# Marking two chains as urgent at once: a retention chunk and an attention block

## The chip, the cores and the metric

The kernel runs on one core of a Trainium2 chip. The metric is the time of one execution on the device in microseconds (us); the time of before is the median of three runs. A core has five engines that run side by side, each with its own queue of instructions that it works off in order: TensorE (PE, matmuls and their weight loads, PEld), VectorE (DVE), ScalarE (ACT), GpSimd (POOL) and SyncE (SP, which issues most transfers). An instruction that waits for a semaphore holds up all that is queued behind it on its engine.

## The reference

The kernel computes a decoder of two layers on one sequence of 1024 tokens with 1024 channels, in float32. Each layer has retention heads and differential attention heads side by side:

```python
u = rmsnorm(h, attn_norm[l])
rq, rk, rv, rg, dq, dk, dv = split(u @ w_in[l])
# retention, chunks of 128, 4 heads of 64 (keys) and 128 (values)
s = einsum(q, k) * decay                  # inside a chunk
out = einsum(s, v) + einsum(q * q_decay, state)
state = g_chunk * state + einsum(k * k_decay, v)
# differential attention, 4 heads, blocks of 128 queries, causal, ALiBi
p = softmax(q_j @ k_j.T * scale - slope * dist)      # j = 0, 1
a = p[0] - lam * p[1]
o = a @ v
h = h + concat(retention, attention) @ w_out[l]
h = h + SwiGLU(rmsnorm(h, ffn_norm[l]))
```

with norms of the outputs of both groups, a gate on retention's, and a last rmsnorm behind the second layer.

## The kernel before, in words

One class, `Trunk`, emits the whole program. Activations lie with channels on the partitions. Matmuls that need the accuracy of float32 are done as three products of a high and a low part (the groups L264 to L266, L288 to L290 and L323 to L325 of the profile). The high part is a copy by ACT, the low part a subtraction by DVE, and so nearly each tile that PE reads has first gone through ACT and then through DVE.

The order of the work. PE's queue is written by hand: the kernel runs under `tc.manual_schedule(engines={PE})`, and generators for different parts are woven together (`weave`), so that PE gets matmuls of projections between the matmuls of an attention block or of a retention chunk. In the feed-forward part the other four engines are ordered by hand too. Everywhere else a scheduler orders the instructions of DVE, ACT, POOL and SP when the program is built: of the instructions that could go next it takes them by their place in the program, and one that was emitted under `tc.high_priority()` may go ahead of the others. The order is then fixed; nothing is decided at run time. PSUM banks come from small pools by name (`ps_s`, `ps_t`, `ps_o`, `ps_mm`), and a matmul group waits until the last reader of its bank is done.

An attention block (`att_block`, one head, 128 queries, key range up to `kend` = 128(i+1)) does this, with points between at which other matmuls are woven in:

1. `att_scores` for the second softmax (j = 1): per 512 keys two matmuls (L574, L575) into a bank `ps_s`; L577 on DVE adds the bias and takes the row maximum (it shows as two instructions, the operation and the reading of its accumulator); L580 the maximum of these, L581 on ACT the exponential with the row sum, L582 the reciprocal of the sum.
2. L656 multiplies the reciprocal by minus lambda, L657 on ACT scales the second softmax by it.
3. `att_scores` for the first softmax (j = 0).
4. `att_turn` for the block before: PE transposes its probabilities (L600) into `ps_t`, ACT copies the high part (L605) and DVE subtracts for the low part (L606).
5. L666 on DVE combines the two softmaxes of this block, reading L657's result.

Each second block `att_out` follows, at the next block: L619 and L620 for the high parts and L622 for the low parts (they read L606's tiles), with the output's norm behind it (`att_norm`: L372, L382, L386 to L388 are the steps of its reciprocal root, and L636 applies it). Between the blocks PE works on the projection of the next head, whose results go through `stack` (L522 on ACT, L523 on DVE), or of the values (L546 on ACT, L547 on DVE).

Already urgent before are L605 and L606, L522 and L523, L666, the copies of `split` and `att_out`, and L869 (`add_h`, the residual sum). L577, L580, L581, L582, L656 and L657 are not.

A retention chunk (`retention`, eight chunks of 128) has the scores (`ret_scores`: matmuls into two `ps_s` banks, L793 twice on DVE for the decay, transposes of the keys, L801 on DVE for the keys' decay), the output (L835 and L838 on PE, L840 and L842 on ACT for its square and its copy), the state's increment (L846 on PE, which reads L801's tile) and its update (L853 on DVE, four times). The chunk before is normed meanwhile (`ret_norm`: L372, L382, L386 to L388, then L809, L811 and L817), and PE gets matmuls of the output projection in between, whose sums L869 adds to the residual.

Of the kernel before, what the change touches and what calls it, by code (L numbers as in the profile page):

```python
# [14 lines left out]
AF = mybir.ActivationFunctionType  # L15
ALU = mybir.AluOpType
AX = mybir.AxisListType

P = 128
# [16 lines left out]
NEG = -3.0e38  # L36
# [111 lines left out]
class Trunk:  # L148
# [413 lines left out]
    def att_scores(self, A, i, j, p, z):  # L562
        nc = self.nc
        qs, ks, kb, bias = A["q"][j], A["k"][j], A["kb"][j], A["bias"]
        kend = P * (i + 1)
        nch = (kend + 511) // 512
        mx = self.t("m", 4, [P, 4])
        q = qs[:, P * i:P * i + P]
        for c in range(nch):
            c0 = 512 * c  # L570
            n = min(512, kend - c0)
            nn = max(n, 256)
            ps = self.bank("s")
            nc.tensor.matmul(ps[:, :nn], lhsT=q, rhs=ks[:, c0:c0 + nn], start=True, stop=False)  # L574
            nc.tensor.matmul(ps[:, :nn], lhsT=q, rhs=kb[:, c0:c0 + nn], start=False, stop=True)  # L575
            x0 = c0 - P * i + (T - P)
            nc.vector.tensor_tensor_reduce(  # L577
                out=p[:, c0:c0 + n], in0=ps[:, :n], in1=bias[:, x0:x0 + n], scale=1.0, scalar=NEG,
                op0=ALU.add, op1=ALU.max, accum_out=mx[:, c:c + 1])
        nc.vector.tensor_reduce(out=mx[:, 2:3], in_=mx[:, 0:nch], op=ALU.max, axis=AX.X, negate=True)  # L580
        nc.scalar.activation(p[:, :kend], p[:, :kend], AF.Exp, bias=mx[:, 2:3], accum_out=z[:, j:j + 1])  # L581
        nc.vector.reciprocal(z[:, 2 + j:3 + j], z[:, j:j + 1])  # L582

    def att_turn(self, A, i, p):
        nc = self.nc
# [53 lines left out]
    def att_block(self, l, A, i, prev):  # L639

        nc = self.nc
        kend = P * (i + 1)
        if i < 4:
            pp = self.big("sp")
            p = [pp[:, 0:512], pp[:, 512:1024]]
        else:
            p = [self.big("sp") for _ in range(2)]
        z = self.t("z", 4, [P, 4])
        self.att_scores(A, i, 1, p[1], z)
        yield LAG[0]  # L650
        if self.outs:
            self.att_out(l, *self.outs.pop())
        elif self.norms:
            self.att_norm(l)
        yield i + LAG[1]
        nc.vector.tensor_tensor(out=z[:, 3:4], in0=z[:, 3:4], in1=self.nlam[:, l:l + 1], op=ALU.mult)  # L656
        nc.scalar.mul(p[1][:, :kend], p[1][:, :kend], z[:, 3:4])  # L657
        self.att_scores(A, i, 0, p[0], z)
        yield i + LAG[2]
        if prev:  # L660
            B, k, q = prev
            self.att_turn(B, k, q)
            if k % 2:
                self.outs.append((B, k // 2))
        with self.tc.high_priority():
            nc.vector.scalar_tensor_tensor(out=p[0][:, :kend], in0=p[0][:, :kend], scalar=z[:, 2:3],  # L666
                                           in1=p[1][:, :kend], op0=ALU.mult, op1=ALU.add)
        yield LAG[3]
        self.prev = (A, i, p)
# [108 lines left out]
    def ret_scores(self, x, n):  # L778
        nc = self.nc
        rq, rk = x[0], x[1]  # L780
        cs = slice(P * n, P * n + P)
        buf = self.big("mx")
        sps = [self.bank("s") for _ in range(2)]
        for h in range(4):
            r = slice(64 * (h % 2), 64 * (h % 2) + 64)
            c0 = P * (h // 2)
            nc.tensor.matmul(sps[h % 2][:, c0:c0 + P], lhsT=rk[h // 2][r, cs], rhs=rq[h // 2][r, cs],
                             start=True, stop=True)
        sd = buf[:, 0:512]
        sdv = sd.rearrange("p (a b c) -> p a b c", a=2, b=2)  # L790
        dec = self.tabs[:, 0:512].rearrange("p (a b c) -> p a b c", a=2, b=2)
        for j in range(2):
            nc.vector.tensor_tensor(out=sdv[:, :, j], in0=sps[j][:, 0:256].rearrange("p (a c) -> p a c", a=2),  # L793
                                    in1=dec[:, :, j], op=ALU.mult)
        kd = buf[:, 512:768]
        if n < 7:
            tps = self.bank("t")
            for p in range(2):
                nc.tensor.transpose(out=tps[:, P * p:P * p + P], in_=rk[p][:, cs], identity=self.ident)
            heads = lambda t: t.rearrange("p (h c) -> p h c", h=4)  # L800
            nc.vector.tensor_tensor(out=heads(kd), in0=heads(tps[:, 0:256]),  # L801
                                    in1=heads(self.tabs[:, 768:772]).broadcast_to([P, 4, 64]), op=ALU.mult)
        return sd, kd

    def ret_norm(self, l, x, mix, n, oc, parts):
# [13 lines left out]
    def retention(self, l, x, mix):  # L819
        nc = self.nc  # L820
        rq, rk, rqd, rv, rg = x
        mm = nc.tensor.matmul
        st = self.t("acc", 2, [P, 512])
        nc.gpsimd.memset(st, 0.0)
        state = [st[:, 0:256], st[:, 256:512]]
        sd, kd = self.ret_scores(x, 0)
        yield 2
        late = None
        for n in range(8):
            cs = slice(P * n, P * n + P)  # L830
            rvn = rv[n // 2][:, 512 * (n % 2):512 * (n % 2) + 512]
            ops = self.bank("o")
            for h in range(4):
                o = ops[:, P * h:P * h + P]
                mm(o, lhsT=rvn[:, P * h:P * h + P], rhs=sd[:, P * h:P * h + P], start=True, stop=n == 0)  # L835
                if n:
                    c0 = P * (h % 2)
                    mm(o, lhsT=state[h // 2][:, c0:c0 + P], rhs=rqd[h // 2][:, cs], start=False, stop=True)  # L838
            sq = self.tmp()
            nc.scalar.activation(sq, ops, AF.Square)  # L840
            oc = sd
            nc.scalar.copy(oc, ops)  # L842
            if n < 7:
                kps = self.bank("t")
                for p in range(2):
                    mm(kps[:, 256 * p:256 * p + 256], lhsT=kd[:, P * p:P * p + P], rhs=rvn[:, 256 * p:256 * p + 256],  # L846
                       start=True, stop=True)
                for p in range(2):
                    for j in range(2):
                        r = slice(64 * j, 64 * j + 64)  # L850
                        kv = kps[r, 256 * p + P * j:256 * p + P * j + P]
                        sv = state[p][r, P * j:P * j + P]
                        nc.vector.scalar_tensor_tensor(out=sv, in0=sv, scalar=self.tabs[r, 772 + p:773 + p], in1=kv,  # L853
                                                       op0=ALU.mult, op1=ALU.add)
            yield 3
            if late:
                self.ret_norm(l, x, mix, *late)
            yield 2
            if n < 7:
                sd, kd = self.ret_scores(x, n + 1)  # L860
            late = (n, oc, self.split(sq))
            yield 3
        self.ret_norm(l, x, mix, *late)
        yield 1
# [439 lines left out]
```

## Time and profile before

| | us |
|---|---|
| median of three runs | 2289.64 (2288.03 to 2290.91) |
| the profiled execution, its own time | 2289.0 |
| span in the profile, first to last instruction | 2287.2 |
| PE busy | 2252.3 (98%) |
| DVE busy | 1397.1 (61%) |
| ACT busy | 1009.7 (44%) |
| POOL busy | 732.6 (32%) |

Attention of layer 0 takes about the stretch from 52 to 300 us, retention that from 382 to 451; in layer 1 the same comes some 1126 us later. A row of the view of waits has the engine, the line that waited, what it waited for, the us in total, how often, and the longest. A row of the timeline has start and length in us, the engine, line, operation and tiles, and in brackets the idle time before it with what ended it.

### The profile page before, as it was taken

Reading aid. Unit: us, or ns where it says so; the run is one execution under the profiler, and the core shown is the slowest. Engines: PE = TensorE matmul, PEld = TensorE weight load, DVE = VectorE, ACT = ScalarE, POOL = GpSimd, SP = SyncE. Lnnn points to the kernel's source line nnn. Section 1 sums busy time; section 2 is a strip of 40 time slices with the busy share of each in tenths; the row PEclk is TensorE's granted clock in tenths of the full one; section 3 lists DMA queues with packets and bytes.
Section 4 is the critical chain, followed back from the end, with each engine's and each line's share of the span. In section 5 each row is a group of like instructions: output and inputs, shape, how many; then the busy total and the mean of one; then the engine's idle time right before and its main releaser. Section 6 shows DMA issues by size and latency. Waiting matters only on the chain.

```text
span 2287.2 us, 30638 instructions
## 1 busy us (share of the span) xinstructions
PE 2252.3 (98%) x11328; PEld 1896.9 (83%) x11328; DVE 1397.1 (61%) x2594; ACT 1009.7 (44%) x1906; POOL 732.6 (32%) x592
## 2 busy tenths in 40 slices
PE   8999999999999999999999999999999999999998
PEld 5888898787888888888888888988878888888887
DVE  8777612989534333895567774059884434359855
ACT  5666623445333333543256665234453333344332
POOL 3111212120445455335121112211214555544350
PEclk9999999999999999999999999999999999999999
DMA  4312121112433332653232222112123232346422
GB/s 166 77 47 65 45 94 38 56 56 65 138 104 103 105 107 92 228 180 99 72 101 56 56 65 87 52 38 74 49 95 120 93 115 93 110 148 201 158 65 74
DMA packets 74214, 216.58 MB, mean 95 GB/s; under 512 B 8016, under 2 KB 10064, under 8 KB 74064
## 3 DMA queue, kind: packets, MB, share of 16 engines
q1 hardware_dynamic: 73488, 214.10, 29.0%
q8 instruction: 89, 1.46, 0.3%
q10 hardware_dynamic: 576, 0.52, 0.1%
q14 instruction: 61, 0.50, 0.1%
HBM read 162.16 MB, written 44.04 MB: 90 GB/s over the span
## 4 chain that ended last, share of the span: by engine, by line
PE 81%; DVE 13%; DMA 2%; ACT 2%; issue 2%; POOL 0%; SPq 0%; DVEq 0%; ACTq 0%; POOLq 0%
PE ps_mm L264 7%; PE ps_mm L265 7%; PE ps_mm L266 7%; PE ps_mm L289 7%; PE ps_mm L288 7%; PE ps_mm L290 7%; PE ps_s L265 4%; PE ps_s L264 4%; PE ps_s L266 4%; PE ps_mm L323 3%; PE ps_mm L324 3%; PE ps_mm L325 3%; PE ps_t L265 2%; PE ps_t L264 2%; PE ps_t L266 2%
## 5 line engine op out<-in xcount | busy, mean ns | idle before, releaser
L241 POOL TENSOR_TENSOR w<-wr,w 128x512 fp32r<-128x512 f32 x262 | 366.7, 1413 | 444.6 <-ACT w L240 426.5
L281 POOL TENSOR_TENSOR w<-wr,w 128x512 fp32r<-128x512 f32 x140 | 186.4, 1338 | 576.9 <-ACT w L280 519.7
L288 PE MATMUL ps_mm<-u,w 128*128 128x512 f32 (+1 forms) x735 | 296.1, 403 | 0.0
L289 PE MATMUL ps_mm<-u,w 128*128 128x512 f32 (+1 forms) x735 | 287.2, 391 | 2.3 <-DVE u L450 2.3
L290 PE MATMUL ps_mm<-u,w 128*128 128x512 f32 (+1 forms) x735 | 286.4, 390 | 0.0
L240 ACT CAST w<-wr 128x512 fp32r<-128x512 f32 x312 | 187.5, 619 | 132.9 <-DVE wr L911 72.5
L264 PE MATMUL ps_mm<-u,w 128*128 128x512 f32 x432 | 168.6, 390 | 0.4 <-DVE a L869 0.3
L266 PE MATMUL ps_mm<-u,w 128*128 128x512 f32 x432 | 168.1, 389 | 0.0
L265 PE MATMUL ps_mm<-u,w 128*128 128x512 f32 x432 | 168.1, 389 | 0.0
L290 PEld LDWEIGHTS ps_mm<-u,w 128*128 128x128 f32 x735 | 138.0, 188 | 30.1
L289 PEld LDWEIGHTS ps_mm<-u,w 128*128 128x128 f32 x735 | 138.6, 189 | 25.7 <-DVE u L450 3.0
L288 PEld LDWEIGHTS ps_mm<-u,w 128*128 128x128 f32 x735 | 138.3, 188 | 23.8
L960 ACT COPY t<-ps_mm 128x512 f32<-128x512 f32 x76 | 44.7, 588 | 240.2 <-PE ps_mm L266 240.2
L280 ACT CAST w<-wr 128x512 fp32r<-128x512 f32 x140 | 85.8, 620 | 128.2 <-PE ps_t L289 39.6
L323 PE MATMUL ps_mm<-w,u 128*128 128x256 f32 x448 | 128.7, 287 | 0.0
L325 PE MATMUL ps_mm<-w,u 128*128 128x256 f32 x448 | 127.6, 285 | 0.0
L324 PE MATMUL ps_mm<-w,u 128*128 128x256 f32 x448 | 127.5, 285 | 0.0
L241 POOL TENSOR_TENSOR w<-t,w 128x512 fp32r<-128x512 f32 x48 | 64.7, 1348 | 193.6 <-ACT w L240 193.5
L577 DVE CUSTOM_DVE_ANT_0 sp<-ps_s,wr 128x512 f32<-128x512 f32 (+2 forms) x192 | 102.9, 552 | 32.2 <-PE ps_s L575 31.3
L581 ACT ACTIVATE sp<-sp,m 128x256 f32<-128x256 f32 (+7 forms) x128 | 99.2, 775 | 50.2 <-DVE m L580 49.4
L869 DVE TENSOR_TENSOR a<-a,ps_mm 128x512 f32<-128x512 f32 (+1 forms) x148 | 98.7, 667 | 29.2 <-PE ps_mm L266 16.2
L909 DVE TENSOR_TENSOR t<-wr,wr 128x512 f32<-128x512 f32 x46 | 34.5, 751 | 116.3 <-DMA wr<-wts 115.5
(390 smaller groups left out, 5915.9 us busy)
## 6 DMA issues: line engine op xcount, KB each, us to landing
wr<-wts SPq DMA_DIRECT2D x190, 512.0 KB, 3.7
mx<-s_fast SPq DMA_DIRECT2D x56, 512.0 KB, 5.0
s_fast<-mx SPq DMA_DIRECT2D x48, 512.0 KB, 4.9
kb<-ka SPq DMA_DIRECT2D x64, 128.0 KB, 2.3
s_rest<-mx SPq DMA_DIRECT2D x12, 512.0 KB, 2.9
kb<-wts SPq DMA_DIRECT2D x12, 512.0 KB, 5.5
mx<-s_rest SPq DMA_DIRECT2D x12, 512.0 KB, 3.2
a<-xT SPq DMA_DIRECT2D x16, 256.0 KB, 5.4
```

Source lines behind the costliest of these rows:

```text
L240: nc.scalar.copy(h, src)
L241: (eng or nc.gpsimd).tensor_tensor(out=o, in0=src, in1=h.bitcast(F32), op=ALU.subtract)
L264: mm(ps, lhsT=wh[:, c], rhs=bh, start=first and i == 0, stop=False, skip_group_check=True)
L265: mm(ps, lhsT=wh[:, c], rhs=bl, start=False, stop=False, skip_group_check=True)
L266: mm(ps, lhsT=wl[:, c], rhs=bh, start=False, stop=i == 3, skip_group_check=True)
L281: nc.gpsimd.tensor_tensor(out=o, in0=raw[:, cols], in1=h.bitcast(F32), op=ALU.subtract)
L288: mm(out, lhsT=lh, rhs=rh, start=first, stop=False)
L289: mm(out, lhsT=lh, rhs=rl, start=False, stop=False)
L290: mm(out, lhsT=ll, rhs=rh, start=False, stop=last)
L323: mm(o, lhsT=uh, rhs=wh, start=k == 0, stop=False)
L324: mm(o, lhsT=uh, rhs=wl, start=False, stop=False)
L325: mm(o, lhsT=ul, rhs=wh, start=False, stop=k == KT - 1)
```

## The change

The change wraps the remaining instructions of the two chains in `tc.high_priority()`. In attention these are L577, L580, L581, L582, L656 and L657; in retention L793, L801, L840, L842 and L853. Since L606, L523, L666 and L869 were urgent before, instructions that used to stand behind these now have the same standing, and their place in the program decides. Nothing is added or removed on any engine, and the orders of PE and SP are the same.

```diff
@@ att_scores
-            nc.vector.tensor_tensor_reduce(
-                out=p[:, c0:c0 + n], in0=ps[:, :n], in1=bias[:, x0:x0 + n], scale=1.0, scalar=NEG,
-                op0=ALU.add, op1=ALU.max, accum_out=mx[:, c:c + 1])
-        nc.vector.tensor_reduce(out=mx[:, 2:3], in_=mx[:, 0:nch], op=ALU.max, axis=AX.X, negate=True)
-        nc.scalar.activation(p[:, :kend], p[:, :kend], AF.Exp, bias=mx[:, 2:3], accum_out=z[:, j:j + 1])
-        nc.vector.reciprocal(z[:, 2 + j:3 + j], z[:, j:j + 1])
+            with self.tc.high_priority():
+                nc.vector.tensor_tensor_reduce(
+                    out=p[:, c0:c0 + n], in0=ps[:, :n], in1=bias[:, x0:x0 + n], scale=1.0, scalar=NEG,
+                    op0=ALU.add, op1=ALU.max, accum_out=mx[:, c:c + 1])
+        with self.tc.high_priority():
+            nc.vector.tensor_reduce(out=mx[:, 2:3], in_=mx[:, 0:nch], op=ALU.max, axis=AX.X, negate=True)
+            nc.scalar.activation(p[:, :kend], p[:, :kend], AF.Exp, bias=mx[:, 2:3], accum_out=z[:, j:j + 1])
+            nc.vector.reciprocal(z[:, 2 + j:3 + j], z[:, j:j + 1])
@@ att_block
-        nc.vector.tensor_tensor(out=z[:, 3:4], in0=z[:, 3:4], in1=self.nlam[:, l:l + 1], op=ALU.mult)
-        nc.scalar.mul(p[1][:, :kend], p[1][:, :kend], z[:, 3:4])
+        with self.tc.high_priority():
+            nc.vector.tensor_tensor(out=z[:, 3:4], in0=z[:, 3:4], in1=self.nlam[:, l:l + 1], op=ALU.mult)
+            nc.scalar.mul(p[1][:, :kend], p[1][:, :kend], z[:, 3:4])
@@ ret_scores
-            nc.vector.tensor_tensor(out=sdv[:, :, j], in0=sps[j][:, 0:256].rearrange("p (a c) -> p a c", a=2),
-                                    in1=dec[:, :, j], op=ALU.mult)
+            with self.tc.high_priority():
+                nc.vector.tensor_tensor(out=sdv[:, :, j], in0=sps[j][:, 0:256].rearrange("p (a c) -> p a c", a=2),
+                                        in1=dec[:, :, j], op=ALU.mult)
...
-            nc.vector.tensor_tensor(out=heads(kd), in0=heads(tps[:, 0:256]),
-                                    in1=heads(self.tabs[:, 768:772]).broadcast_to([P, 4, 64]), op=ALU.mult)
+            with self.tc.high_priority():
+                nc.vector.tensor_tensor(out=heads(kd), in0=heads(tps[:, 0:256]),
+                                        in1=heads(self.tabs[:, 768:772]).broadcast_to([P, 4, 64]), op=ALU.mult)
@@ retention
-            nc.scalar.activation(sq, ops, AF.Square)
             oc = sd
-            nc.scalar.copy(oc, ops)
+            with self.tc.high_priority():
+                nc.scalar.activation(sq, ops, AF.Square)
+                nc.scalar.copy(oc, ops)
...
-                        nc.vector.scalar_tensor_tensor(out=sv, in0=sv, scalar=self.tabs[r, 772 + p:773 + p], in1=kv,
-                                                       op0=ALU.mult, op1=ALU.add)
+                        with self.tc.high_priority():
+                            nc.vector.scalar_tensor_tensor(out=sv, in0=sv, scalar=self.tabs[r, 772 + p:773 + p],
+                                                           in1=kv, op0=ALU.mult, op1=ALU.add)
```

The lines of the changed kernel are numbered otherwise: L577 is L578 there, L580 is L582, L582 is L584, L606 is L608, L622 is L624, L636 is L638, L656 is L659, L666 is L669, L793 is L797, L801 is L806, L853 is L860 and L869 is L876. The numbers behind the tiles' names are the program's counts of buffers and banks.

The first place is on DVE at the end of head 0's block 6 in layer 0: `sp_923` and `sp_924` are that block's softmaxes, `sp_1017` that of the block behind it, `a_179_901` and `a_180_902` the low parts of the transposed block before, and `mx_464` the head's output. Before:

```order
L606 TENSOR_TENSOR a_179_901<-ps_t_1000,a_177_899 128x4x128
L606 TENSOR_TENSOR a_180_902<-ps_t_1007,a_178_900 128x2x128
L577 ISA sp_1017,m_1019<-ps_s_1020,wr_467 128x512
L577 ISA m_1019 128x1
L577 ISA sp_1017,m_1019<-ps_s_1024,wr_467 128x512
L577 ISA m_1019 128x1
L523 SCALAR_TENSOR_TENSOR a_105_469<-ps_mm_967,a_105_469 64x512
L582 RECIPROCAL z_925<-z_925 128x1
L580 TENSOR_REDUCE m_1019<-m_1019 128x1
L666 SCALAR_TENSOR_TENSOR sp_923<-sp_923,z_925,sp_924 128x896
```

And in the changed kernel:

```order
L669 SCALAR_TENSOR_TENSOR sp_923<-sp_923,z_925,sp_924 128x896
L578 ISA sp_1017,m_1019<-ps_s_1020,wr_467 128x512
L578 ISA m_1019 128x1
L578 ISA sp_1017,m_1019<-ps_s_1024,wr_467 128x512
L578 ISA m_1019 128x1
L608 TENSOR_TENSOR a_180_902<-ps_t_1007,a_178_900 128x2x128
L582 TENSOR_REDUCE m_1019<-m_1019 128x1
L523 SCALAR_TENSOR_TENSOR a_105_469<-ps_mm_967,a_105_469 64x512
L608 TENSOR_TENSOR a_179_901<-ps_t_1000,a_177_899 128x4x128
```

The combination of the softmaxes has gone from the end to the front, and the first of the two L606 from the front to the end; the instructions up to the last row are the same in both. In head 2's block 6 the same rows change places.

The second place is on DVE at head 1's block 6 in layer 0: `sp_1515` and `sp_1516` are its softmaxes, `a_307_1496` and `a_308_1497` the low parts of the block before, `t_318_1533` and `t_319_1535` belong to the norm of the head's output. Before:

```order
L606 TENSOR_TENSOR a_307_1496<-ps_t_1570,a_305_1494 128x4x128
L606 TENSOR_TENSOR a_308_1497<-ps_t_1577,a_306_1495 128x2x128
L386 TENSOR_TENSOR t_318_1533<-t_318_1533,t_319_1535 128x512
L580 TENSOR_REDUCE m_1547<-m_1547 128x1
L577 ISA sp_1587,m_1589<-ps_s_1590,wr_1124 128x512
L577 ISA m_1589 128x1
L387 TENSOR_TENSOR t_318_1533<-t_318_1533,t_319_1535 128x512
L577 ISA sp_1587,m_1589<-ps_s_1594,wr_1124 128x512
L577 ISA m_1589 128x1
L388 SCALAR_TENSOR_TENSOR t_319_1535<-t_318_1533,t_319_1535 128x512
```

And in the changed kernel:

```order
L578 ISA sp_1587,m_1589<-ps_s_1590,wr_1124 128x512
L578 ISA m_1589 128x1
L578 ISA sp_1587,m_1589<-ps_s_1594,wr_1124 128x512
L578 ISA m_1589 128x1
L608 TENSOR_TENSOR a_307_1496<-ps_t_1570,a_305_1494 128x4x128
L582 TENSOR_REDUCE m_1589<-m_1589 128x1
L669 SCALAR_TENSOR_TENSOR sp_1515<-sp_1515,z_1517,sp_1516 128x896
L523 SCALAR_TENSOR_TENSOR a_225_1127<-ps_mm_1418,a_225_1127 64x512
L608 TENSOR_TENSOR a_308_1497<-ps_t_1577,a_306_1495 128x2x128
```

Both L606 stand behind the two L577 of the next scores, the second of them also behind L666 and an L523, and the norm's L386 to L388 come later still.

The third place is on DVE in retention's chunk 2 in layer 0: `ps_s_4067` and `ps_s_4068` hold its scores, `ps_t_4075` its transposed keys, `t_732_4048` and `t_733_4050` belong to the norm of the chunk before. Before:

```order
L372 TENSOR_TENSOR t_739_4081<-t_728_4024,t_738_4079 128x512
L386 TENSOR_TENSOR t_732_4048<-t_732_4048,t_733_4050 128x512
L793 TENSOR_TENSOR mx_4066<-ps_s_4067,c_tabs 128x2x128
L869 TENSOR_TENSOR a_698_3908<-a_698_3908,ps_mm_4041 128x512
L387 TENSOR_TENSOR t_732_4048<-t_732_4048,t_733_4050 128x512
L793 TENSOR_TENSOR mx_4066<-ps_s_4068,c_tabs 128x2x128
L388 SCALAR_TENSOR_TENSOR t_733_4050<-t_732_4048,t_733_4050 128x512
L801 TENSOR_TENSOR mx_4066<-ps_t_4075,c_tabs 128x256
```

And in the changed kernel:

```order
L372 TENSOR_TENSOR t_739_4081<-t_728_4024,t_738_4079 128x512
L797 TENSOR_TENSOR mx_4066<-ps_s_4067,c_tabs 128x2x128
L797 TENSOR_TENSOR mx_4066<-ps_s_4068,c_tabs 128x2x128
L806 TENSOR_TENSOR mx_4066<-ps_t_4075,c_tabs 128x256
L876 TENSOR_TENSOR a_698_3908<-a_698_3908,ps_mm_4041 128x512
L386 TENSOR_TENSOR t_732_4048<-t_732_4048,t_733_4050 128x512
L387 TENSOR_TENSOR t_732_4048<-t_732_4048,t_733_4050 128x512
L388 SCALAR_TENSOR_TENSOR t_733_4050<-t_732_4048,t_733_4050 128x512
```

The two L793 and L801 go ahead of the residual sum and of the norm's three steps.

## The prediction

> **What bounds the kernel now.** I read the head of the page first, for the share of each engine.
>
> ```profile
> span 2287.2 us, 30638 instructions
> PE 2252.3 (98%) x11328; PEld 1896.9 (83%) x11328; DVE 1397.1 (61%) x2594; ACT 1009.7 (44%) x1906; POOL 732.6 (32%) x592
> PE 81%; DVE 13%; DMA 2%; ACT 2%; issue 2%; POOL 0%; SPq 0%; DVEq 0%; ACTq 0%; POOLq 0%
> ```
>
> TensorE (PE) is busy in 98% of the span, and 81% of the chain that ended last is its work. Its instructions are written in a fixed order that the change leaves as it is, so a new order on the other engines can only shorten or lengthen the moments in which PE stands. The view of waits, for PE alone, tells where these are (line, what it waited for, us in total, times, longest):
>
> ```profile
> PE ps_mm L289 <- DVE u L450: 2.3, 2, 1.4
> PE ps_o L835 <- DVE mx L793: 2.2, 4, 1.0
> PE ps_s L574 <- DVE z L656: 1.9, 2, 0.9
> PE ps_t L600 <- DVE sp L666: 1.4, 2, 0.7
> PE ps_t L846 <- DVE mx L801: 0.6, 2, 0.3
> PE ps_s L574 <- DVE m L577: 0.4, 2, 0.2
> ```
>
> The last five rows are all of PE's waits on the two chains that the change marks: 2.2 + 1.9 + 1.4 + 0.6 + 0.4 = 6.5 us, 0.28% of the span, in pairs (or four) because each occurs once per layer. More than that the change can't gain. What it can lose has no such ceiling: any VectorE (DVE) instruction that now comes later than PE's use of it makes a new wait.
>
> **The change, part by part.** Nothing is added or taken away. PE's and SyncE's orders are the same word for word, so no matmul, load or store moves past another, and no DMA is issued in another place. What moves is the place of DVE instructions, by 1 to 15, some ScalarE (ACT) instructions by up to 7, and a few of GpSimd. So each edit costs nothing by itself, and what is left is to step through the new DVE order with the durations of the old trace and ask at each move whether PE waits. I did this for one layer; the other has the same moves.
>
> *Gain in retention.* Chunk 2 of layer 0, DVE and then PE (start, us, engine, line, tile, shape, and in brackets the idle time before):
>
> ```profile
> 398.26 0.68 DVE L386 TENSOR_TENSOR t<-t,t 128x512 f32<-128x512 f32 x1
> 399.20 0.68 DVE L869 TENSOR_TENSOR a<-a,ps_mm 128x512 f32<-128x512 f32 x1
> 399.80 1.34 DVE L387 TENSOR_TENSOR t<-t,t 128x512 f32<-128x512 f32 x1
> 401.06 0.41 DVE L793 TENSOR_TENSOR mx<-ps_s,c_tabs 128x256 f32<-128x256 f32 x1
> ...
> 401.52 0.49 PE L835 MATMUL ps_o<-mx,v 128*128 128x128 f32 x2 [0.95 <-DVE mx L793]
> ```
>
> The second L793 stood behind three longer instructions, 2.7 us with them; now it goes directly behind the first, ahead of L386, L869 and L387. Its PE wait of 0.95 us goes whole. So do the waits for L801 (0.3) and the smaller one for L793: (2.2 + 0.6)/2 = 1.40 us per layer. The pushed norm (L386 to L388) feeds only the output half a chunk later; L869 frees a PSUM bank, and it is pushed by two instructions of 0.4. I take no new wait there.
>
> *Gain in attention.* The 0.9 us wait that the view puts to L656 is really for the bank that the 128-wide L577 ahead of it reads; that L577 moves four places up, ahead of an L523 and an L606. That wait and the 0.2 us wait for L577 go: (1.9 + 0.4)/2 = 1.15 us per layer. Together the gains are 2.55 us per layer.
>
> *Loss 1, at the end of head 0's block 6.* The low half of the transposed probabilities (L606) was urgent before, and the scores around it were not; now all of them are. Old times, DVE and then PE:
>
> ```profile
> 97.56 1.02 DVE L606 TENSOR_TENSOR a<-ps_t,a 128x512 fp32r<-128x512 f32 x2
> 98.49 0.68 DVE L577 CUSTOM_DVE_ANT_0 sp<-ps_s,wr 128x512 f32<-128x512 f32 x1
> ...
> 99.83 0.69 DVE L523 SCALAR_TENSOR_TENSOR a<-ps_mm,a 64x512 fp32r<-64x512 f32 x1
> ...
> 100.74 1.15 DVE L666 SCALAR_TENSOR_TENSOR sp<-sp,z,sp 128x896 f32<-128x896 f32 x1
> 101.92 0.69 DVE L523 SCALAR_TENSOR_TENSOR a<-ps_mm,a 64x512 fp32r<-64x512 f32 x1
> ...
> 100.11 0.88 PE L622 MATMUL ps_o<-a,v 128*128 128x256 f32 x6
> ...
> 92.00:101.90 9.90, 9.70 (x24) 1.00 0.35 89
> ```
>
> The group at 97.56 is two L606; the first writes the 128x512 tile that the first L622 reads. In the new order this one stands behind L666, both L577, the other L606, L580 and the first L523. That is to say: the instructions up to and with it are now the very ones that ended before with L666, with L606 last in place of L666. DVE has no room to do them sooner, since it was busy 9.70 of the 9.90 us (last row: stretch, its length, DVE busy, PE clock, DMA). So this L606 ends where L666 ended, at about 101.86, and PE, which reaches L622 at 100.11, stands 1.75 us. Had DVE filled its 0.20 us of idle time the wait would be 1.55; if L666's inputs come late, it is longer.
>
> *Loss 2, the same place of head 2.*
>
> ```profile
> 211.36 1.02 DVE L606 TENSOR_TENSOR a<-ps_t,a 128x512 fp32r<-128x512 f32 x2
> ...
> 214.54 1.15 DVE L666 SCALAR_TENSOR_TENSOR sp<-sp,z,sp 128x896 f32<-128x896 f32 x1
> ...
> 212.98 0.88 PE L622 MATMUL ps_o<-a,v 128*128 128x256 f32 x6
> ...
> 206.60:215.70 9.10, 8.94 (x23) 1.00 0.46 115
> ```
>
> The same swap with the same set: L606 ends where L666 ended, 214.54 + 1.15 = 215.69 less the 0.03 by which neighbours overlap, and PE stands from 212.98: 2.7 us (2.5 with DVE's idle filled).
>
> *Loss 3, head 1's block 6.* Here the later L606 of the two falls behind L666, but four others leave the set:
>
> ```profile
> 147.87 0.68 DVE L386 TENSOR_TENSOR t<-t,t 128x512 f32<-128x512 f32 x1
> ...
> 149.14 0.69 DVE L387 TENSOR_TENSOR t<-t,t 128x512 f32<-128x512 f32 x1
> ...
> 150.35 1.18 DVE L388 SCALAR_TENSOR_TENSOR t<-t,t 128x512 f32<-128x512 f32 x1
> ...
> 151.58 0.74 DVE L636 SCALAR_TENSOR_TENSOR mx<-mx,c_dg,t 128x512 f32<-128x512 f32 x1
> 152.24 1.14 DVE L666 SCALAR_TENSOR_TENSOR sp<-sp,z,sp 128x896 f32<-128x896 f32 x1
> 149.44 0.88 PE L622 MATMUL ps_o<-a,v 128*128 128x256 f32 x6
> ```
>
> L666 ended at 153.38; less 0.68 + 0.69 + 1.18 + 0.74 = 3.29 the set ends at 150.1, or 150.4 with the overlaps left in. The fifth of the six L622 is the first to read this L606, at 149.44 + 4/6 of the 0.7 us that they take = 149.9. The wait is 0.2 us at least; it is 1.1 if L666 waits for ACT's L657, which now has two L605 ahead of it. I take 0.75.
>
> *Two small losses.* In head 1's block 3 L666 goes behind two reciprocals, a maximum and L656, three places; in head 2's block 1 it goes behind two L577 and L547:
>
> ```profile
> 127.51 0.15 DVE L582 RECIPROCAL z<-z 128x1 f32<-128x1 f32 x1
> 180.05 0.55 DVE L577 CUSTOM_DVE_ANT_0 sp<-ps_s,wr 128x384 f32<-128x384 f32 x1
> 179.97 0.38 PE L600 MATMUL ps_t<-c_ident,sp 128*128 128x128 f32 x2
> ```
>
> The first has a wait already, the 0.7 us of L600, and three such instructions of up to 0.15 us add 0.2 to 0.45 to it: I take 0.3, and that wait stays. The second ends, by the argument of the set, no later than the L577 at 180.05 did, 180.6, and L600 wants it at 179.97: 0 to 0.6, and I take 0.45 as there is idle time ahead of it that doesn't all fill.
>
> *The sum.* Losses 1.75 + 2.7 + 0.75 + 0.3 + 0.45 = 5.95 us per layer, gains 2.55, net 3.4, twice 6.8 us. The profiled execution took 2289.0 us (1.8 us lie around the span), so 2295.8; the median of the runs is 0.6 higher, which gives 2296.4. With all low bounds (1.55 + 2.5 + 0.2 + 0.2 + 0 = 4.45) it is 2293.4, with the high ones (1.95 + 2.7 + 1.1 + 0.45 + 0.6 = 6.8) 2298.1.
>
> **The rivals.** *A: the clock falls.* New waits are longer than any that the middle of the kernel has, and once, near the start, a long wait was followed by a slow clock (stretch, length, busy time of five engines, PE clock, DMA):
>
> ```profile
> 27.22 1.84 PE L398 MATMUL ps_s<-c_ones,acc 128*128 128x1 f32 x8 [2.95 <-DVE acc L433]
> 28.00:38.00 10.00, 9.07 (x41) 8.57 (x42) 9.72 (x17) 5.02 (x10) 4.84 (x4) 0.54 0.44 125
> 1154.00:1156.00 2.00, 1.99 (x9) 1.64 (x10) 1.15 (x2) 0.59 (x1) 0.00 (x0) 1.00 0.87 277
> ```
>
> After 2.95 us without a matmul the granted clock was 0.54 for ten us, a loss of 10 x 0.46 = 4.6 us; after the 1.4 us wait for L450 it stayed at 1.00. Loss 2's 2.7 us lie between these, and nearer to the former. One such drop in each layer adds 9.2 us: 2305.6. [...]
>
> *B: faster.* The mechanism is at loss 1 and 2: the urgent scores reach ACT's exponential sooner, and ACT hands L666 its inputs sooner, so DVE reaches L606 ahead of PE after all. It decides at 100.11 and 212.98: DVE would have to be 1.75 and 2.7 us further on than it was. Then the gains alone are left, with loss 3 and the small ones absent too: 2 x 2.55 = 5.1, 2284.5; if the wait for L666 goes as well, 2289.6 - 6.5 = 2283.1. Against it stands that DVE had only 0.20 and 0.16 us of idle time in these two stretches.
>
> *C: no change.* The losses come to about 2.55 us per layer, less than half of what I stepped, because PE's position shifts against DVE's or because an order read from the program doesn't come out as the old durations say: 2289.6. For it: each loss rests on a margin of one or two DVE instructions. Against: the largest of them alone is 2.7.
>
> **How the numbers follow.** Forecast as summed 0.55, A 0.13, B 0.12, C 0.20. What a measurement of this kernel can tell from no change is about 0.2%, 4.6 us: B lies on the faster side, the forecast and A on the slower, C within. So faster 0.12, same 0.20, slower 0.68. The range must leave out no more than 2 in 10: it gives up B (0.12) and the upper half of A, and runs from 2286 to 2305. The forecast's own range is 2293 to 2298. I round the time to 2296.5.
>
> **What would show it.** In the profile after, PE's waits should lack L835 <- L793, L846 <- L801 and the 0.9 us of L574; this confirms the gains. There should be a row of L622 waiting for DVE's L606 (608 in the new numbering), about four in all of 1.75 and 2.7 us, near 100 and 213 us and at the same two places of layer 1; without this row the forecast is wrong and B or C holds. A clock below 1.00 in the stretch behind 213 says A. If waits appear on lines that I gave nothing (L869's banks, the norms), the step "no new wait there" has failed.

## The result and the profile after

The changed kernel took 2308.34 us (median of 4 runs, 2306.27 to 2310.80) against 2289.87 us (4 runs): 1.008 times, 95% interval 1.0067 to 1.0092. That is 18.5 us slower, where 6.8 were forecast; the sign was right, the size was not, and the time lies above the range. The profiled execution has a span of 2309.0 us against 2287.2, 21.8 more.

PE's instructions are as before; its busy time is 4.7 us longer, as a lower clock lengthens some of them (behind the first of the new waits below, the 128x512 matmuls L288 to L290 start every 0.43 us at a clock of 0.50 and every 0.23 at 1.00). The head of the page after has more DVE time for the same number of instructions, 12.3 us of it.

```profile
PE 2257.0 (98%) x11328; PEld 1898.8 (82%) x11328; DVE 1409.4 (61%) x2594; ACT 1010.1 (44%) x1906; POOL 731.2 (32%) x592
PE 77%; DVE 14%; ACT 3%; issue 2%; DMA 2%; POOL 0%; DVEq 0%; SPq 0%; ACTq 0%; POOLq 0%
```

The view of waits for PE, after (line, what it waited for, us in total, times, longest; the line numbers are those of the changed kernel):

```profile
PE ps_o L624 <- DVE a L608: 10.9, 6, 2.3
PE ps_o L840 <- DVE mx L797: 4.9, 4, 1.5
PE ps_t L602 <- DVE sp L669: 3.7, 2, 1.9
PE ps_t L379 <- ACT t L370: 1.8, 2, 0.9
PE ps_t L602 <- DVE m L582: 0.7, 2, 0.3
PE ps_t L380 <- DVE t L372: 0.5, 2, 0.2
```

The first row is the new wait for the low half of the turned probabilities, three places per layer. The old waits at L574 and for L801 are gone. But L840's wait for the decayed scores, which should have gone, has grown from 2.2 to 4.9 us, and L379 and L380 in retention's norm wait where they had not. In the two chains together: 10.9 + (3.7 - 1.4) + 0.7 - (1.9 + 0.4) = 11.6 us in attention, and (4.9 - 2.2) + 1.8 + 0.5 - 0.6 = 4.4 us in retention.

Loss 1's place after, on DVE and then on PE:

```profile
99.96 1.14 DVE L669 SCALAR_TENSOR_TENSOR sp<-sp,z,sp 128x896 f32<-128x896 f32 x1
101.14 0.69 DVE L578 CUSTOM_DVE_ANT_0 sp<-ps_s,wr 128x512 f32<-128x512 f32 x1
...
102.36 0.42 DVE L608 TENSOR_TENSOR a<-ps_t,a 128x256 fp32r<-128x256 f32 x1
...
103.59 0.69 DVE L608 TENSOR_TENSOR a<-ps_t,a 128x512 fp32r<-128x512 f32 x1
...
104.34 0.86 PE L624 MATMUL ps_o<-a,v 128*128 128x256 f32 x5 [1.94 <-DVE a L608]
```

It came as stepped: L608 is the last of the set, DVE works without a pause, and PE stands 1.94 us. What the step did not price is the clock behind some of these waits (stretch, its length, busy time of five engines, PE clock):

```profile
105.00:110.00 5.00, 5.00 (x18) 3.97 (x17) 1.07 (x2) 1.29 (x2) 0.00 (x0) 0.66 0.02 3
222.00:228.00 6.00, 5.65 (x28) 4.82 (x29) 2.68 (x9) 3.41 (x7) 0.46 (x1) 1.00 0.10 20
1240.00:1246.00 6.00, 5.80 (x28) 4.96 (x29) 2.54 (x9) 3.43 (x5) 0.60 (x1) 1.00 0.11 24
1356.00:1362.00 6.00, 5.24 (x19) 4.31 (x20) 1.73 (x5) 2.66 (x5) 0.00 (x0) 0.72 0.00 1
```

Behind the first and the fourth of the four long waits the clock was below full for a few us, a loss of 5 x 0.34 = 1.7 and 6 x 0.28 = 1.7 us; behind the second and third it was not.

### The profile page after: what moved, and what is told of

Its sections match the earlier page's. It is cut to its first block, busy times and chain, and to the rows that moved or that the text cites. A ratio compares the mean times of both kernels' runs of the same rounds, so it can differ in the third digit from the quotient of the medians.

```text
span 2309.0 us, 30642 instructions
## 1 busy us (share of the span) xinstructions
PE 2257.0 (98%) x11328; PEld 1898.8 (82%) x11328; DVE 1409.4 (61%) x2594; ACT 1010.1 (44%) x1906; POOL 731.2 (32%) x592
## 4 chain that ended last, share of the span: by engine, by line
PE 77%; DVE 14%; ACT 3%; issue 2%; DMA 2%; POOL 0%; DVEq 0%; SPq 0%; ACTq 0%; POOLq 0%
PE ps_mm L264 7%; PE ps_mm L265 7%; PE ps_mm L266 7%; PE ps_mm L289 6%; PE ps_mm L288 6%; PE ps_mm L290 6%; PE ps_s L265 4%; PE ps_s L264 4%; PE ps_s L266 4%; PE ps_mm L325 3%; PE ps_mm L323 3%; PE ps_mm L324 3%; PE ps_t L265 2%; PE ps_t L264 2%; PE ps_t L266 2%
## 5 line engine op out<-in xcount | busy, mean ns | idle before, releaser
L281 POOL TENSOR_TENSOR w<-wr,w 128x512 fp32r<-128x512 f32 x140 | 185.5, 1331 | 584.4 <-ACT w L280 524.6
L288 PE MATMUL ps_mm<-u,w 128*128 128x512 f32 (+1 forms) x735 | 297.1, 404 | 0.0
L290 PE MATMUL ps_mm<-u,w 128*128 128x512 f32 (+1 forms) x735 | 287.7, 391 | 0.0
L290 PEld LDWEIGHTS ps_mm<-u,w 128*128 128x128 f32 x735 | 138.6, 189 | 30.5
L288 PEld LDWEIGHTS ps_mm<-u,w 128*128 128x128 f32 x735 | 138.7, 189 | 24.0
L578 DVE CUSTOM_DVE_ANT_0 sp<-ps_s,wr 128x512 f32<-128x512 f32 (+2 forms) x192 | 101.7, 554 | 42.8 <-PE ps_s L575 41.3
L876 DVE TENSOR_TENSOR a<-a,ps_mm 128x512 f32<-128x512 f32 (+1 forms) x148 | 98.7, 667 | 29.2 <-PE ps_mm L266 16.1
```

The lines of the kernel that those rows point to most:

```text
L281: nc.gpsimd.tensor_tensor(out=o, in0=raw[:, cols], in1=h.bitcast(F32), op=ALU.subtract)
L288: mm(out, lhsT=lh, rhs=rh, start=first, stop=False)
L290: mm(out, lhsT=ll, rhs=rh, start=False, stop=last)
```

## The experiments

Theory H: attention's loss is the standing of L608 among instructions that are urgent too. Theory F: in retention DVE has no time to spare, so what PE wins at chunks 2 and 4 it gives back, and more, at chunks 5 to 7. The rivals: retention's new waits follow from attention's disorder (P), the losses would move to another wait if L608 were helped (S), and the lengths that single DVE instructions get beside GpSimd make retention's waits alone (G).

**Each half alone.** `e_att` has the change's hunks of attention only, `e_ret` those of retention only.

> Only the attention half of the change. Theory H (the halves add, each loses by itself): PE's new waits in attention, 1.94 + 2.18 + 1.27 + 1.15 + 0.35 us less 1.15 us of old ones that go, are 5.7 us per layer, so 2289.9 + 11.5 = 2301.4, and up to 3.2 us more where the clock drops behind a wait; PE's waits for L608 sum to 10 to 11.5 us in six places, and retention keeps the waits of before (0.95, 0.29, 0.16 us). Rival P (retention's new waits are a consequence of attention's disorder, through weights or banks that come later): the waits of 0.9 and 1.5 us at retention's chunks 5 and 6 show up here too, and the time is near 2306.

> Only the retention half of the change. Theory F (VectorE is full there: what PE wins at chunk 2 and 4 it gives back at chunk 5 to 7, and the pushed norm loses more): the waits of 0.95 and 0.29 us go, waits of about 0.9, 1.5 and 1.1 us come at chunks 5, 6 and in the norm behind, +1.6 us per layer, 2289.9 + 3.2 = 2293. Rival P (as forecast, alone it gains 1.40 us per layer; the new waits came from attention's half): 2287.1 and no wait over 0.3 us on L840 at chunks 5 and 6.

Measured: 2304.15 us, 1.0064 (1.0050 to 1.0077), for attention alone and 2293.57 us, 1.0016 (1.0008 to 1.0025), for retention alone. With 2289.90 in these runs the two are 14.3 and 3.7 us slower, 17.9 together against 18.5 for the whole. PE's waits in the stretch of layer 0's retention, of the kernel before, of `e_ret` and of the whole change:

```profile
PE ps_o L835 <- DVE mx L793: 1.1, 2, 1.0
PE ps_t L846 <- DVE mx L801: 0.3, 1, 0.3
```

```profile
PE ps_o L837 <- DVE mx L794: 2.4, 2, 1.5
PE ps_t L379 <- ACT t L370: 0.9, 1, 0.9
PE ps_t L380 <- DVE t L372: 0.2, 1, 0.2
```

```profile
PE ps_o L840 <- DVE mx L797: 2.5, 2, 1.5
PE ps_t L379 <- ACT t L370: 0.9, 1, 0.9
PE ps_t L380 <- DVE t L372: 0.2, 1, 0.2
```

Retention's half makes its new waits alone, and `e_att` has the old ones there unchanged. P falls: the halves add.

**L608 ahead of all.** `e_turn` is the whole change with one more edit, which puts the turned copies (L607, L608) ahead of the rest of the urgent work:

```diff
-            with self.tc.high_priority():
+            with self.tc.high_priority(offset=10**6):
                 nc.scalar.copy(dh, pv)
                 nc.vector.tensor_tensor(out=dl, in0=pv, in1=dh.bitcast(F32), op=ALU.subtract)
```

> The whole change, with the copies of the turned probabilities (L607, L608 of the changed kernel) set ahead of all other urgent work. Theory H (L608 stood behind L669 and the scores, and that is all that PE waited for in three places per layer): PE's waits for L608, 10.9 us, go, and with them the two clock drops of 1.7 and 1.5 us; retention's waits stay: 2308.3 - 14.1 = 2294. Rival S (the same work is only shifted: what L608 overtakes, L669 or L578, is now what PE waits for): at least half of the 10.9 us comes back as waits for L669 or in L574, 2300 or more.

Measured: 2295.09 us, 1.0022 (1.0013 to 1.0030), 13.2 us less than the whole change. Loss 1's place in this run:

```profile
99.37 1.02 DVE L608 TENSOR_TENSOR a<-ps_t,a 128x512 fp32r<-128x512 f32 x2
...
101.55 0.88 PE L624 MATMUL ps_o<-a,v 128*128 128x256 f32 x6
```

And PE's waits on the chain in layer 0's attention (60 to 300 us):

```profile
PE ps_t L602 <- DVE sp L669: 1.9, 1, 1.9
PE ps_s L574 <- DVE m L578: 0.9, 2, 0.5
PE ps_o L621 <- ACT a L607: 0.2, 1, 0.2
```

No L624 waits for L608, and the clock is at 1.00 in these places. L574 waits 0.9 us again, far less than half of what went. So H holds and S is a small part of the truth. Attention's mark gains nothing even so: 3.0 us of waits per layer here, against 1.8 in the kernel before (0.9 + 0.7 + 0.2 in the same view).

**Less work for DVE in retention.** `e_gate` is the retention half without the gate's product:

```diff
-        nc.vector.tensor_tensor(out=oc, in0=oc, in1=rg[n // 2][:, 512 * (n % 2):512 * (n % 2) + 512], op=ALU.mult)
```

> The retention half of the change, with one VectorE instruction per chunk of the norm left out (the gate's product, 0.69 us; its result is missing from the output). Theory F (VectorE is full): with 0.7 us less per chunk VectorE keeps up with PE, the waits at chunks 5 and 6 fall below 0.4 us together and the ones of before stay away: about 2.0 us per layer less than the retention half alone, 2289. Rival G (only the length that single VectorE instructions get beside GpSimd's makes these waits): the load is not what matters, and the two waits stay above 1.5 us together, 2292.

Measured: 2284.91 us, 0.9977 (0.9968 to 0.9987), and PE waits for nothing in layer 0's retention, neither at the old places nor the new. That is 8.7 us less than `e_ret`, and the waits that went are 4.9 + 1.8 + 0.5 = 7.2 of it, in both layers together. F's waits went as expected, and the time fell 4 us further than it said. But the run doesn't refute G. From the first decay product to the last in layer 0's retention, six of DVE's instructions in `e_ret` took 1.0 to 1.7 us where their median is 0.69, 4.4 us more in all; in `e_gate` four did, 2.1 us more, about as in the kernel before (three, 2.2 us). Two of the three longest, the norm's last subtraction, had their usual length in `e_gate`. So this run took away both DVE's work and some of the lengthening, and can't tell F from G.

**GpSimd quiet.** `e_pool` is the whole change with GpSimd's subtraction for the weights' low parts left out:

```diff
             nc.scalar.copy(h, raw[:, cols])
-            nc.gpsimd.tensor_tensor(out=o, in0=raw[:, cols], in1=h.bitcast(F32), op=ALU.subtract)
+            nc.scalar.copy(o, raw[:, cols])
```

> The whole change, with GpSimd's subtraction for the low part of most weights (L281) left out: ScalarE copies the weights in its place, so the low parts are wrong. Theory G (VectorE instructions between tiles in SBUF are lengthened while GpSimd runs, 0.69 to 1.7 us, and that sizes the misses): L669 in head 1's block 3 takes under 1.0 us where it took 1.65, its wait of 1.87 us falls to 0.9 to 1.2; retention's waits of 0.9 and 1.5 us fall to under 1.2 together; L608's waits stay at 10 to 11 us; 2308.3 - 1.6 - 2.6 = 2304, down to 2302. Rival O (the order alone makes the waits): all of them stay within 0.3 us, 2308.

Measured: 2287.96 us, 0.9990 (0.9981 to 0.9999), 20 us less than the whole change: G's direction at nearly five times its size. PE doesn't wait in layer 0's retention at all, although the order of DVE's instructions there is the same as in the changed kernel. The reason is in the lengths: two instructions of the changed kernel beside GpSimd's, then a group of the norm's steps (times in ns: shortest, median, longest) there and in `e_pool`.

```profile
444.29 1.72 DVE L822 TENSOR_TENSOR u<-mx,u 128x512 fp32r<-128x512 f32 x1
444.17 1.29 POOL L281 TENSOR_TENSOR w<-wr,w 128x512 fp32r<-128x512 f32 x1 [13.36 <-ACT w L280]
...
132.04 1.65 DVE L669 SCALAR_TENSOR_TENSOR sp<-sp,z 128x384 f32<-128x384 f32 x1
132.00 1.26 POOL L281 TENSOR_TENSOR w<-wr,w 128x512 fp32r<-128x512 f32 x1 [9.65 <-ACT w L280]
...
L822 DVE TENSOR_TENSOR u<-mx,u x16: 683/692/1716, 415.5 to 1616.6; 128x512 fp32r<-128x512 f32 x16
```

```profile
L822 DVE TENSOR_TENSOR u<-mx,u x16: 683/692/693, 408.4 to 1595.3; 128x512 fp32r<-128x512 f32 x16
...
128.36 0.62 DVE L669 SCALAR_TENSOR_TENSOR sp<-sp,z 128x384 f32<-128x384 f32 x1
```

An L822 that starts 0.12 us into an L281 ends 0.55 us behind it (446.01 against 445.46); alone it takes 0.69 us. Without L281 the longest L822 is 693 ns, and the L669 of the small loss takes 0.62 us where it took 1.65. The residual sums L876, which read one input from PSUM, are not lengthened: in the changed kernel the 112 of them that ran beside a GpSimd instruction took 0.69 us at most, and so did the other 136. So the lengthening is needed for retention's new waits: the same order without it makes none. Whether it would be enough if DVE had less to do, no run shows. In head 2's block 6 the order of `e_pool` differs (one L608 stands some places earlier, and the wait there is 0.4 us; L608's waits, which should have stayed at 10 to 11 us, come to 6.3), so its total is not a price of GpSimd alone; PE's waits for L450 ahead of the projections (2.2 + 1.4 us in the changed kernel) are gone in it as well. In loss 1's and loss 3's places the order is the same, and PE waits 1.88 and 1.25 us as before: those two losses are the order's alone.

**A version that keeps the gain.** If DVE lacks time in retention, ACT (busy 22.5 us of the 50 in a row below) can take the scaling of the norm's sum, which reads PSUM. First everywhere, with no mark (`c_act0`), with retention's half (`c_act`), with `e_turn` (`c_all`), and with the whole change without the edit of `e_turn` (`c_noturn`):

```diff
-        nc.vector.tensor_scalar(out=x, in0=ps, scalar1=-0.5 / dim, scalar2=-0.5 * EPS, op0=ALU.mult, op1=ALU.add)
+        nc.scalar.activation(x, ps, AF.Copy, scale=-0.5 / dim, bias=-0.5 * EPS)
```

> The kernel before, with the scaling of the norm's sum (L382, 0.69 us on VectorE) done by ScalarE. Theory F (retention is bound by VectorE's load): the waits of 0.95, 0.29 and 0.16 us per layer shrink by half or more, 2289.9 - 1.4 to 2.8 = 2287 to 2288.5. Rival A (it is ScalarE's chain that counts, and it gets longer): waits on L370 or L385 appear, 2290 or more.

> The retention half of the change, with the same scaling on ScalarE. Theory F: with 0.7 us less on VectorE per chunk the marked chain keeps what it wins, as in the run without the gate's product: no wait over 0.3 us on L840's line in retention, 2289.9 - 2.8 - (the rest of what VectorE is spared) = 2285 to 2287. Rival A (ScalarE's part of the norm now stands behind the urgent square and copy): new waits for L370, 2289 or more.

> The whole change with the turned copies ahead of all and the scaling on ScalarE. If retention's waits go as in the run before this one, 2295.1 less about 7 us of them, 2288; attention's own waits (1.9 us at L602, 0.4 and 0.5 us at L574) stay, so it doesn't beat the retention half alone. If attention, too, was short of VectorE, L602's wait falls below 1.2 us and the time to 2285.

> The whole change with L382 on ScalarE everywhere, the turned copies as they were. Theory H (the copies' standing is what costs in attention): waits for L608 of several us per layer return against the run with them ahead (2285.2), 2292 to 2298. Rival: a VectorE with less to do has the copies done in time anyway, and it is within 2 us of 2285.2.

Measured: `c_act0` 2301.46 us, 1.0051 (1.0038 to 1.0063); `c_act` 2290.57, 1.0003 (0.9994 to 1.0012); `c_all` 2285.17, 0.9979 (0.9970 to 0.9988); `c_noturn` 2297.91, 1.0032 (1.0021 to 1.0044). `c_act0` refuted both of its expectations: with less for DVE to do, PE waits more in retention than before. Its waits in layer 0's retention, and DVE ahead of the worst of them:

```profile
PE ps_o L835 <- DVE mx L793: 3.3, 3, 1.6
PE ps_t L846 <- DVE mx L801: 1.1, 1, 1.1
```

```profile
423.48 0.68 DVE L387 TENSOR_TENSOR t<-t,t 128x512 f32<-128x512 f32 x1
424.08 0.68 DVE L869 TENSOR_TENSOR a<-a,ps_mm 128x512 f32<-128x512 f32 x1
424.68 1.48 DVE L388 SCALAR_TENSOR_TENSOR t<-t,t 128x512 f32<-128x512 f32 x1
426.08 0.41 DVE L793 TENSOR_TENSOR mx<-ps_s,c_tabs 128x256 f32<-128x256 f32 x1
```

The order has changed: three longer instructions stand ahead of the second L793. With the mark (`c_act`) the second L793 is not behind them, and PE does not wait in retention at all. So with this edit the mark in retention is worth 4.4 us of waits per layer against this order. Its time was still above the 2285 to 2287 expected; what `c_act` loses is in attention, whose order the edit shuffled as well (waits of 1.4 and 2.2 us per layer, and a lower clock behind the longer one in both layers, 1.7 us each). `c_noturn` against `c_all` shows H again, about 12 us by the ratios (1.0032 against 0.9979), with waits for L608 of 8.5 us in all and a lower clock behind three of the four, 5.1 us.

**The same in retention's norm alone**, so that attention's DVE order is not shuffled, with retention's half (`c_ret`) and with `e_turn` (`c_both`):

```diff
+        if tag == "t":
+            nc.scalar.activation(x, ps, AF.Copy, scale=-0.5 / dim, bias=-0.5 * EPS)
+        else:
             nc.vector.tensor_scalar(out=x, in0=ps, scalar1=-0.5 / dim, scalar2=-0.5 * EPS, op0=ALU.mult, op1=ALU.add)
```

> The retention half of the change, with L382 on ScalarE in retention's norm alone, so that attention's order is the one of before. Theory F (retention is short of VectorE time, attention's order was the trouble of the runs that moved L382 everywhere): no wait on L840's line over 0.2 us in retention, attention's waits as before (1.87 us per layer): 2289.9 - 2.8 - up to 1 = 2286 to 2287. Rival: ScalarE's longer chain makes waits at L379 and L380 of 0.4 us or more per layer, 2288 to 2289.

> The whole change with the turned copies ahead of all, and L382 on ScalarE in retention's norm alone. Retention's waits of 3.6 us per layer go (theory F), attention's stay as in the run with the turned copies ahead: 2295.1 - 7 = 2288. If it is below 2286, attention's mark is worth something by itself; if it is 2288 or more, the better of the two earlier versions stays the one with L382 on ScalarE everywhere (2285.2).

Measured: `c_ret` 2285.48 us, 0.9976 (0.9967 to 0.9985), and `c_both` 2287.64, 0.9987 (0.9978 to 0.9996), against 2290.53 in these runs. In `c_ret` PE waits for nothing in layer 0's retention; its stretch from 407 to 457 us, and that of the kernel before (busy time of PE, PEld, DVE, ACT, POOL):

```profile
407.00:457.00 50.00, 50.00 (x287) 41.52 (x286) 45.45 (x80) 26.45 (x48) 10.31 (x8) 1.00 0.17 54
```

```profile
407.00:457.00 50.00, 49.50 (x281) 40.70 (x281) 45.79 (x82) 22.51 (x40) 9.42 (x7) 1.00 0.17 52
```

ACT has taken the work, and PE is busy without a break. DVE is busy 45.5 us of this stretch, hardly less than the 45.8 before, so its share alone does not tell a chunk with waits from one without. `c_ret` and `c_all` both beat the kernel before and the changed one; they can't be told apart. `c_ret` is the smaller edit: no mark in attention.

## Why the prediction was right or wrong, point by point

**The gains.** Both in attention came whole: no wait at L574 is left of the 2.3 us. Those in retention at chunks 2 and 4 came too, and were given back.

**Losses 1, 2 and 3: the mechanism was right.** Per layer 1.75, 2.7 and 0.75 us were forecast; 1.94, 2.18 and 1.27 came in layer 0, and 1.93, 2.34 and 1.28 in layer 1. The argument that a set of instructions ends when it ended before, whatever its order, held to half a microsecond. That the sum of the three came so close (5.2 forecast, 5.39 and 5.55 measured) is luck in part: loss 2 came below its bounds of 2.5 to 2.7 and loss 3 above its bounds of 0.2 to 1.1, and the two misses nearly cancel. `e_turn` shows that the new standing is the cause. With waits at these places, rivals B and C fall.

**The small losses.** The one at L600 was forecast to add 0.3 us to 0.72 and added 1.15: three short instructions more ahead of L669 were right, but they also moved it under an L281 of GpSimd, and it took 1.65 us in place of 0.99. `e_pool` shows it. The other came to 0.35 for 0.45.

**"I take no new wait there", for retention: the step that failed.** Forecast was a gain of 1.40 us per layer; the half alone lost 3.7 us in both layers, 1.8 per layer. The step asked of each moved instruction whether anyone waits for it, with the durations of the old trace. It did not ask how long each takes beside its new neighbours, nor whether DVE had time for the whole chunk. The prediction's own sign for this, waits in the norms, came with L379 and L380. The same stretch of chunk 5 before and after, on DVE and then on PE:

```profile
433.46 1.06 DVE L853 SCALAR_TENSOR_TENSOR acc<-acc,c_tabs,ps_t 64x128 f32<-64x128 f32 x3
434.44 0.68 DVE L817 TENSOR_TENSOR u<-mx,u 128x512 fp32r<-128x512 f32 x1
...
436.85 0.75 DVE L793 TENSOR_TENSOR mx<-ps_s,c_tabs 128x256 f32<-128x256 f32 x2
...
439.00 0.38 PE L835 MATMUL ps_o<-mx,v 128*128 128x128 f32 x2
```

```profile
442.83 1.42 DVE L860 SCALAR_TENSOR_TENSOR acc<-acc,c_tabs,ps_t 64x128 f32<-64x128 f32 x4
...
447.24 0.74 DVE L797 TENSOR_TENSOR mx<-ps_s,c_tabs 128x256 f32<-128x256 f32 x2
...
447.80 0.46 PE L840 MATMUL ps_o<-mx,v 128*128 128x128 f32 x2 [0.91 <-DVE mx L797]
```

PE is ready for L840 at 446.89, 7.89 us later than before, and DVE starts the chunk's updates 9.37 us later: it has lost 1.5 us against PE. Some 0.8 us of that is lengthening (up to here four of the chunks' instructions are 2.4 us over their medians together, against two and 1.6 us before); the rest is part of the 1.4 us that PE had won. Before, DVE was done about 1.5 us ahead of PE here, so the 1.5 us only use that up. From there to L797 takes 4.41 us against 3.39, and the L822 of 1.72 us in place of 0.69 is the 1.0 between them: this makes the wait of 0.91 us. In 407 to 457 us DVE was busy 45.8 of 50 us in the kernel before; that row, shown above, was a warning that there was little time to lose. Without the lengthening, in the same order, every wait in retention is gone (`e_pool`); with 0.7 us less work per chunk they are gone too (`e_gate`), but with part of the lengthening. So the lengthening is shown to be needed, and that the full load is needed too is argued.

**Rival A, the clock,** was given 4.6 us for each drop and a chance of 0.13, apart from the forecast. It came together with the forecast: two drops of 1.7 us among four long waits. It should have been a term of the sum, and a smaller one: a drop lasts 3.41 us here, and the ten us that it was priced by were three of these on end (10.24 us at a clock of 0.50, from 27.01 us on).

**The rest.** Of the 11.7 us between the forecast of 6.8 and the 18.5 measured, retention has 6.5 (a gain of 2.8 forecast, a loss of 3.7 in `e_ret`) and attention 4.7 (9.6 forecast, 14.3 in `e_att`). In the trace of `e_att` the clock falls behind two waits, 3.4 us, and L669's wait is 0.85 us per layer longer than forecast. Between the two traces, 11.6 + 4.4 + 3.4 = 19.4 of the 21.8 us are read above; the traced run is the longest of its four. About 2 us more are gone by 40 us of the span, where the instructions of PE, DVE, ACT and POOL stand in the same order in both kernels: 1.7 of them are one more stretch of 3.41 us at half clock, from 16.8 us on, which `e_ret` has too, so they are not laid on the change.

## What to carry to other kernels

Urgent is a place in a row: what is marked competes first with what was urgent already, so list those instructions and give the one with the least time before its reader the higher standing. Ahead of pulling one chain forward, read how busy the engine is over the whole stretch; where it is busy nine tenths of it (45.8 of 50 us here), little is left to take up anything that gets longer, and a wait removed early can come back later. And a swap of order can be priced by the set argument, but each new neighbour can change an instruction's length (here DVE's L822 took 1.72 us beside GpSimd's L281 and 0.69 without it): look for instructions in the old trace that take twice their median.

## What the runs showed of the hardware

In the changed kernel a DVE instruction with both inputs in SBUF, L822, took up to 1.72 us beside a GpSimd instruction that reads SBUF, L281, and 0.69 without GpSimd; the residual sums L876, with one input in PSUM, took 0.69 at most either way.

Waits of PE of 1.9 us were followed by a lower clock, though not each time: in the changed kernel 1.94 us was and 1.93 us was not, 2.34 us was and 2.18 us was not. In the run of attention's half the two waits of 1.93 us were, and those of 2.34 and 2.24 us were not:

```profile
103.00:109.00 6.00, 5.23 (x19) 4.29 (x20) 1.72 (x5) 2.67 (x5) 0.00 (x0) 0.72 0.08 17
221.00:227.00 6.00, 5.09 (x25) 4.36 (x26) 3.22 (x10) 3.41 (x7) 0.00 (x0) 1.00 0.03 5
1237.00:1243.00 6.00, 5.87 (x22) 4.83 (x23) 1.73 (x7) 2.05 (x3) 0.00 (x0) 0.72 0.00 0
1355.00:1361.00 6.00, 5.79 (x28) 4.95 (x29) 2.54 (x9) 3.42 (x5) 0.60 (x1) 1.00 0.11 24
```

In the traces of the kernel before and of the changed one the granted clock falls to 0.50 for 3.41 us, for 10.24 us on end near the start, and from near the end of the span on. Within a trace these stretches start whole multiples of 3.413 us apart: in the changed kernel at 16.82, 30.47, 105.56, 1358.25 and 2300.33 us (4, 22, 367 and 276 between), in the kernel before at 27.01 and 2279.81 us (660). So each of the two traces can be laid out in windows of 3.41 us, and the time that PE stands can be added up in each. From 60 to 2200 us of the changed kernel there are two windows in which PE stood 1.92 us or more, and each was followed by a window at half clock; the next longest, 1.84 us, was not. In the kernel before, none of these windows has more than 0.95 us, and none was followed by half clock. In the first 60 us it is otherwise: there a window at half clock came behind one in which PE stood 1.01 us in the changed kernel, and behind one of 0.21 us in the kernel before.

For the four long waits of the changed kernel the length did not decide; their place in the windows did. Loss 1's 1.94 us in layer 0 lay in one window (102.15 to 105.56 us), and so did 1.92 of loss 2's 2.34 us in layer 1 (1354.84 to 1358.25 us). Loss 2's 2.18 us in layer 0 were cut into 1.45 and 0.73 by the edge at 221.61 us, loss 1's 1.93 us in layer 1 into 0.51 and 1.42 by the edge at 1238.79 us. In the run of attention's half loss 1's 1.93 us in layer 1 were followed by the drop, so the place in the program alone doesn't tell. Whether the edges move from one execution of the same kernel to the next was not shown: each kernel has one trace. A window at half clock costs 1.7 us, half of its 3.41 us.
